# An encoder layer on one core: second chunk's squares first, third chunk's first weights on GpSimd's queue, late adaLN tiles beside the attention, last blocks' halves in turn

## The chip, the cores and the metric

The kernel runs on one core of a Trainium2 chip. A core has a matmul engine (TensorE, PE), VectorE (DVE), ScalarE (ACT), GpSimd (POOL) and SyncE (SP), which run side by side, each through its own program in order, and wait for each other by semaphores; DMA engines move data between the core's SBUF and memory. The metric is the time of one execution on the device in microseconds, lower is better. The kernel before was run three times, with 2073.9, 2080.23 and 2075.73 us (median 2075.73).

## The reference

One layer of an encoder on 2048 tokens of width 1024, all in fp32: modulated RMSNorm, windowed attention with 16 query heads, 4 key heads, a sink logit and a relative bias, then a SwiGLU feed-forward (FFN) of hidden width 2816. Shift, scale and gate of each half come from a vector `c` by one matrix (adaLN).

```python
mod = silu(c) @ ada_w + ada_b            # 6 x 1024: shift, scale, gate for two halves
h = rmsnorm(x) * (1 + scale1) + shift1
q, k, v = split(h @ w_qkv)
logits = q @ k_band.T / 8 + bias         # each block of 128 queries sees 3 blocks of keys
p = softmax(concat([masked(logits), sink]))[..., :-1]
x = x + gate1 * rmsnorm((p @ v_band) @ w_o)
h2 = rmsnorm(x) * (1 + scale2) + shift2
gate, up = split(h2 @ w_in)
x = x + gate2 * rmsnorm((silu(gate) * up) @ w_out)
```

## The kernel before

Every fp32 factor is split in a high and a low part (`split`, lines 149 to 151: ScalarE casts, another engine subtracts), and a product is three matmuls (`three`, L145 to L147). The tokens are worked on in four chunks of 512 with the features on the partitions.

By time: up to about 65 us the first chunk's norm, and its first seven QKV tiles (`NORD[:WAVE]`) one input tile k after the other, as the weights land. To 172.6 the rest of the first chunk and all of the second, with both sets of weights resident: `w1`-pool tiles hold the first seven tiles' columns (printed `w0_k`), `w2` the other five (printed `w1_k`). To about 783 the attention: 64 units (four chunks, four key heads, four blocks of 128 queries), each a score step (`scores`: matmuls L509, softmax L512 on VectorE, L514 on ScalarE, L518 on GpSimd) and, two units later, a value step (`values`: transposes L531, matmuls L536 and L537). Between units a generator gives 17.9 matmuls' worth of filling work (`Budget`): the QKV of the third and fourth chunk (`fill_qkv`, weights loaded again as `wsr`, split to `ws`), then the output projection of finished blocks (`TokenBlock`). To about 1640 the FFN's first matrix, by blocks of seven products of sums (`Hidden`, `Block.step`), in two halves of 1024 tokens; then the second matrix to the end.

A scheduler puts each engine's program in an order of its own, by a timeline that it keeps; `tc.issue_after(x)` holds an instruction back behind `x` in that order, and pools decide what memory a tile shares with earlier ones. SP issues nearly all loads and stores, and at most eight of its DMAs are under way, since eight semaphores go round: a DMA waits until the one eight before, SP's or ScalarE's, has landed.

What the change touches:

- `Chunk.squares` (L176): ScalarE squares eight tiles, two engines in turn add them up (L186). For the second chunk it is called behind the seven evacuations and behind the second set of weights (`w_piece(k, 1)`, splits on GpSimd, L151). `norm` sums over the features by matmuls with ones (`nsta`, L121), either on the fp32 sums (`direct`) or on a split of them.
- `late_ada` (L380): 24 adaLN tiles of 512 KB beyond the first 16 are loaded on GpSimd's queue beside the QKV of two chunks, and reduced on VectorE (L298).
- The pools of the attention (L428): the bias tables lie in memory opened first, the probability buffers `pr` after them. GpSimd clears `pr` (L456).
- `last_blocks` (L842): the last two token blocks of the output projection, two halves of 24 matmuls each, block after block, and behind each block its two RMSNorms and stores of `x1_d` and `n_d` (`ends`, on ScalarE's queue).
- `give_pair` (L911): from two hidden tiles by two halves it makes the operands of the second matrix; two of its subtractions (L934, L938) run on GpSimd.

Of the kernel before, what the change touches and what calls it, by code (L numbers as in the profile page):

```python
# [17 lines left out]
P = 128  # L18
# [49 lines left out]
def encoder_layer(ctx, tc, a):  # L68
# [190 lines left out]
    with ExitStack() as pa:  # L259
# [37 lines left out]
        def ada_reduce(t, w):  # L297
            dve.tensor_tensor_reduce(w, w, cb, 1.0, adab[:, t:t + 1], ALU.mult, ALU.add, mod[:, t:t + 1])  # L298
# [26 lines left out]
        for k in range(KT):  # L325
            with tc.issue_after(steps[max(k - 2, 0)][0]) if k >= 1 else ExitStack():
                ada_reduce(*ada_load(8 + k, raws))
                shift = ada_load(k, raws)
                w_piece(k, 0)
            with tc.issue_after(steps[k - 1][1]) if k >= 1 else ExitStack():  # L330
                ada_reduce(*shift)
            dve.scalar_tensor_tensor(coef[:, 0, k:k + 1], mod[:, 8 + k:9 + k], 1.0, gains[:, 0, k:k + 1],
                                     ALU.add, ALU.mult)
            with tc.issue_after(steps[k - 2][1]) if k >= 2 else ExitStack():
                steps.append(ch0.h(k))
            for n in NORD[:WAVE]:
                three(pss[n], wres[k, n], ch0.hh[k], k == 0, k == KT - 1)
        for n in NORD[:WAVE]:
            evac(0, n, pss[n], psA, "mm")
# [5 lines left out]
        ch1 = Chunk(1)  # L345
        ch1.squares()

# [31 lines left out]
        waiting, left = [], list(range(2 * KT, 5 * KT))  # L379

        def late_ada(n, keep):
            with tc.issue_after(newest["norm"]):
                while len(waiting) > keep:
                    ada_reduce(*waiting.pop(0))
            for _ in range(min(n, len(left))):
                waiting.append(ada_load(left.pop(0), raws, pool))

        for i, n in enumerate(NORD[WAVE:]):
            qkv_tile(ch0, n)
            if i == 0:  # L390
                ch1.norm(psA, "mm", True)
            if i >= 1:
                ch1.h(2 * i - 2)
                ch1.h(2 * i - 1)
            if i >= 2:
                late_ada(2 + (i == 4), 2)
        for i, n in enumerate(NORD):
# [5 lines left out]
            if i == 5:  # L403
                ch2.norm(psA, "mm")
# [24 lines left out]
    qkv = open_pool(att, "qkv", 2, side="right")  # L429
    bp = open_pool(att, "bp", side="right")  # L430
    sm = open_pool(att, "sm", 4, side="right")
    pp = open_pool(att, "pp", side="right")
# [113 lines left out]

    def fill_qkv(ch, nxt):

        for i, n in enumerate([8, 9, 10, 11] + list(range(8))):
            ni = NORD.index(n)  # L550
            raw = wsr.tile([P, KT, P], F32, tag="raw", name=f"wsr{ch.c}_{n}")
            newest["wsr"] = sp.dma_start(raw, a["w_qkv"][:, :, ni * P:(ni + 1) * P].rearrange("k p c -> p k c")).ins
# [9 lines left out]
            if nxt is not None:  # L562
                if i == 0:
                    with tc.issue_after(newest["wsr"]):
                        nxt = nxt()
# [206 lines left out]

    units = [Unit(c, g, jb) for c in range(NCH) for g in range(KVH) for jb in range(JB)]
# [27 lines left out]
    weights = output_weights()  # L801
    for i, un in enumerate(units):
# [3 lines left out]
        if un.jb == 0 and i + JB < len(units):  # L806
            nx = units[i + JB]
            load_qkv(nx.c, nx.g)
        if 22 <= i < half:
            next(weights, None)  # L810
# [31 lines left out]
    def last_blocks(bs):  # L842

        blocks = [TokenBlock(NCH - 1, b, late=True) for b in bs]
        for x in blocks:
            for i in range(2):
# [4 lines left out]
            x.ends()  # L851
# [60 lines left out]
    def give_pair(hf, j):  # L912
# [19 lines left out]
        b11, b12, b21, b22 = (b[n] for n in ("b11", "b12", "b21", "b22"))  # L932
        give("b11", b11, True)
        pool.tensor_tensor(b11, b12, b11, ALU.subtract)  # L934
# [3 lines left out]
        pool.tensor_tensor(b22, b22, b11, ALU.subtract)  # L938
# [424 lines left out]
```

## Time and profile before

| | |
|---|---|
| profiled execution | 2078.2 us, its span 2076.4 |
| mean granted TensorE clock | 0.989 of full speed |
| TensorE busy | 2017.2 us, 97% of the span, 9412 matmuls |
| VectorE, ScalarE, GpSimd busy | 1505.6, 992.5 and 921.8 us |
| DMA | 398.49 MB, 192 GB/s in the mean |
| chain that ended last | TensorE 72%, VectorE 9%, DMA 9%, ScalarE 4% |

A busy share of TensorE counts a matmul that waits in its pipe as busy, so TensorE does less work in a stretch than it could even where little idle time shows. The granted clock has two levels, 1.2 GHz (0.5) and 2.4 GHz (1.0). In a table of stages each engine has its busy time with the number of its instructions; in a group by shape the columns are line, engine, operation, output and inputs, shapes and count, then busy time and the mean of one in ns, then the idle time before them and what ended it. A chain of waits is followed back from the end of a stretch: each piece has its start and length.

### The profile page before, as it was taken

The page shows a single profiled execution, that of the slowest core. Times are in us where ns is not written, and L with a number is a line of the kernel's source. Part 1 is how long each engine was busy: PE and PEld are TensorE (multiplying, and loading weights), DVE is VectorE, ACT ScalarE, POOL GpSimd, SP SyncE. Part 2 cuts the span into 40 slices and gives each one's busy share as a digit, 9 for nine tenths or more (in the row PEclk, how much of TensorE's full clock was granted, in tenths as well). Part 3 has the DMA queues.
Part 4 walks back from the last instruction along what each step waited for, and adds up shares of the span by engine and source line. Part 5 has one row for each costly group of instructions (what it writes and reads, how often), then busy time and mean ns, then how long its engine had stood idle before and what let it go on. Part 6 is the DMA issues. An engine that isn't in the chain of part 4 may idle for free.

```text
span 2076.4 us, 28772 instructions
## 1 busy us (share of the span) xinstructions
PE 2017.2 (97%) x9412; PEld 1660.0 (80%) x9412; DVE 1505.6 (73%) x2632; ACT 992.5 (48%) x2105; POOL 921.8 (44%) x915
## 2 busy tenths in 40 slices
PE   8898999999999998999999999999999999999998
PEld 6786788878887786888888887888888788888886
DVE  8767566657777668566676698777776699987656
ACT  4426667667777656333233343434333554453222
POOL 0414556444445635555665456545553333344300
PEclk9999999999999999999999999999999999999999
DMA  7889678674647575433743454544534454488663
GB/s 299 261 259 270 177 195 252 154 194 138 200 141 229 183 246 193 145 130 108 245 161 121 159 173 149 203 146 158 187 137 149 155 179 147 152 310 343 254 253 122
DMA packets 256645, 398.49 MB, mean 192 GB/s; under 512 B 85045, under 2 KB 135781, under 8 KB 254448
## 3 DMA queue, kind: packets, MB, share of 16 engines
q1 hardware_dynamic: 245776, 363.03, 53.8%
q0 software_dynamic: 4928, 16.85, 2.3%
q10 hardware_dynamic: 5792, 16.79, 2.1%
q8 instruction: 74, 1.21, 0.2%
q14 instruction: 75, 0.61, 0.1%
HBM read 267.83 MB, written 128.76 MB: 191 GB/s over the span
## 4 chain that ended last, share of the span: by engine, by line
PE 72%; DVE 9%; DMA 9%; ACT 4%; issue 3%; POOL 2%; SPq 1%; DVEq 0%; ACTq 0%; POOLq 0%
PE pc_i L147 12%; PE pc_i L146 12%; PE pc_i L145 12%; PE po L1215 5%; PE po L1216 5%; PE po L1217 5%; PE psq L147 3%; PE psq L145 3%; PE psq L146 3%; PE t L531 2%; PE s L509 2%; PE py L624 1%; PE py L625 1%; PE py L626 1%; PE o L537 1%
## 5 line engine op out<-in xcount | busy, mean ns | idle before, releaser
L145 PE MATMUL pc_i<-ht,ws_i 128*128 128x512 f32 x528 | 206.7, 392 | 4.9 <-ACT ht L150 4.9
L146 PE MATMUL pc_i<-ht,ws_i 128*128 128x512 f32 x528 | 207.3, 393 | 1.6 <-DVE ht L151 1.6
L147 PE MATMUL pc_i<-ht,ws_i 128*128 128x512 f32 x528 | 207.2, 392 | 0.0
L150 ACT CAST wa_i<-wiri 128x512 fp32r<-128x512 f32 x132 | 81.6, 620 | 217.0 <-DMA wiri<-w_in 118.1
L512 DVE CUSTOM_DVE_ANT_0 pr<-s,bias,nsink 128x288 f32<-128x288 f32 (+3 forms) x256 | 125.0, 500 | 81.5 <-PE s L509 70.0
L518 POOL TENSOR_SCALAR pr<-pr,rs 128x288 f32<-128x288 f32 (+3 forms) x256 | 130.3, 528 | 113.3 <-DVE rs L516 107.8
L514 ACT ACTIVATE pr<-pr,nm 128x289 f32<-128x289 f32 (+3 forms) x256 | 135.4, 531 | 60.6 <-DVE nm L512 54.9
L890 POOL TENSOR_TENSOR s_i<-wiri 128x512 f32<-128x512 f32 x44 | 61.0, 1387 | 197.7 <-DMA wiri<-w_in 168.2
L151 DVE TENSOR_TENSOR wa_i<-wiri,wa_i 128x512 fp32r<-128x512 f32 x132 | 128.1, 970 | 24.3 <-ACT wa_i L150 24.1
L1220 DVE TENSOR_TENSOR z<-po,z 128x512 f32<-128x512 f32 x164 | 110.7, 684 | 44.4 <-PE po L1217 42.6
L151 DVE TENSOR_TENSOR ws_i<-s_i,ws_i 128x512 fp32r<-128x512 f32 x132 | 127.1, 963 | 21.1 <-ACT ws_i L150 20.9
L145 PE MATMUL pc_i<-hb,wa_i 128*128 128x512 f32 x352 | 138.1, 392 | 0.0
L147 PE MATMUL pc_i<-hb,wa_i 128*128 128x512 f32 x352 | 137.7, 391 | 0.0
L146 PE MATMUL pc_i<-hb,wa_i 128*128 128x512 f32 x352 | 137.5, 391 | 0.0
L151 DVE TENSOR_TENSOR plo<-t,phi 128x512 fp32r<-128x512 f32 x184 | 122.0, 680 | 20.1 <-ACT phi L150 19.6
L1215 PE MATMUL po<-wo_s,g 128*128 128x512 f32 x320 | 124.2, 391 | 2.4 <-DVE z L1220 1.7
L1216 PE MATMUL po<-wo_s,g 128*128 128x512 f32 x320 | 124.8, 390 | 0.1
L1217 PE MATMUL po<-wo_s,g 128*128 128x512 f32 x320 | 124.5, 389 | 0.0
L531 PE MATMUL t<-ident,pr 128*128 128x128 f32 x736 | 118.4, 276 | 5.9 <-POOL pr L518 3.4
L509 PE MATMUL s<-k,q 128*128 128x288 f32 (+4 forms) x512 | 114.3, 319 | 9.3 <-DVE nm L512 7.7
L145 PEld LDWEIGHTS pc_i<-ht,ws_i 128*128 128x128 f32 x528 | 99.7, 189 | 27.2 <-ACT ht L150 5.3
L146 PEld LDWEIGHTS pc_i<-ht,ws_i 128*128 128x128 f32 x528 | 99.7, 189 | 23.7 <-DVE ht L151 1.9
(255 smaller groups left out, 5913.3 us busy)
## 6 DMA issues: line engine op xcount, KB each, us to landing
wiri<-w_in SPq DMA_DIRECT2D x88, 512.0 KB, 4.7
wr<-w_out SPq DMA_DIRECT2D x20, 1024.0 KB, 9.0
g<-g_d_t SPq DMA_DIRECT2D x36, 512.0 KB, 5.2
g<-g_d_b SPq DMA_DIRECT2D x35, 512.0 KB, 5.7
q_d<-eq SPq DMA_DIRECT2D x64, 256.0 KB, 5.0
q<-q_d SPq DMA_DIRECT2D x16, 1024.0 KB, 9.0
ada<-ada_w POOLq DMA_DIRECT2D x24, 512.0 KB, 6.4
wsr<-w_qkv SPq DMA_DIRECT2D x24, 512.0 KB, 5.4
```

The source lines that it names most:

```text
L145: pe.matmul(ps, w[0], h[0], start=first, stop=False)
L146: pe.matmul(ps, w[0], h[1], start=False, stop=False)
L147: pe.matmul(ps, w[1], h[0], start=False, stop=last)
L151: return eng.tensor_tensor(lo, src, f(hi), ALU.subtract).ins
L509: m = pe.matmul(ps[:, :n], qs, kk[:, e, jb * P + lo:jb * P + hi], start=e == 0, stop=e == 1)
L512: dve.tensor_tensor_reduce(pr[:, i, lo:hi], ps[:, :n], bias[g][:, lo - starts[i]:hi - starts[i]], -1.0, nsink[:, g:g + 1], ALU.add, ALU.mi ...
L514: act.activation(pr[:, i, lo:hi + 1], pr[:, i, lo:hi + 1], AF.Exp, bias=nm[:, i:i + 1], scale=-1.0, accum_out=rs[:, i:i + 1])
L518: pool.tensor_scalar(pr[:, i, lo:hi], pr[:, i, lo:hi], rs[:, i:i + 1], 1.0, ALU.mult, ALU.mult)
L531: pe.transpose(pt[:, i * P:(i + 1) * P], pr[:, i, jj * P:(jj + 1) * P], ident)
L1215: pe.matmul(ps, g[:, 0], w[:, 0], start=i < FRESH and k == 0, stop=False, **on)
L1216: pe.matmul(ps, g[:, 0], w[:, 1], start=False, stop=False, **on)
L1217: pe.matmul(ps, g[:, 1], w[:, 0], start=False, stop=k == m - 1, **on)
```

## The change

1. The second chunk's squares are added before the evacuations of the first seven tiles and before the second weights, all on GpSimd.
2. Eight of the 24 late adaLN tiles are loaded on SP into two buffers and reduced by a generator that is stepped beside every second unit from the fourth on; the other 16 wait for an earlier norm.
3. The third chunk's norm sums the fp32 squares directly.
4. `pr` is opened before the bias tables, so `pr` now lies over the first weights and the bias over the second.
5. The weights of the third and fourth chunk come from a copy in memory of another layout (`w_qkv_t`, 4 KB in one piece for each partition); the first two tiles, 8 and 9, go on GpSimd's queue ahead of the units. The fourth chunk is no longer held behind the second weight tile.
6. The last two blocks' halves are made in turn.
7. Where an operand is given in two parts, which is in the second half of the tokens, both GpSimd subtractions go to VectorE.

```diff
+        ch1 = Chunk(1)
+        ch1.squares((pool, pool))
         for n in NORD[:WAVE]:
             evac(0, n, pss[n], psA, "mm")
...
         for k in range(KT):
             w_piece(k, 1)
-        ch1 = Chunk(1)
-        ch1.squares()
...
-        waiting, left = [], list(range(2 * KT, 5 * KT))
+        waiting, left = [], list(range(2 * KT, 4 * KT))
         def late_ada(n, keep):
-            with tc.issue_after(newest["norm"]):
+            with tc.issue_after(first_norm[0]):
...
-                ch2.norm(psA, "mm")
+                ch2.norm(psA, "mm", True)
...
+    pp = open_pool(att, "pp", side="right")
     bp = open_pool(att, "bp", side="right")
     sm = open_pool(att, "sm", 4, side="right")
-    pp = open_pool(att, "pp", side="right")
...
+    def raw_weights(c, n, q=sp):
+        ni = NORD.index(n)
+        raw = wsr.tile([P, KT, P], F32, tag="raw", name=f"wsr{c}_{n}")
+        ins = q.dma_start(raw, a["w_qkv_t"][ni]).ins
+        if q is sp:
+            newest["wsr"] = ins
+        return raw
+
+    ahead_of_units = {(2, n): raw_weights(2, n, pool) for n in (8, 9)}
...
                 if i == 0:
-                    with tc.issue_after(newest["wsr"]):
-                        nxt = nxt()
+                    nxt = nxt()
...
+    def ada_beside():
+        todo = list(range(4 * KT, 5 * KT))
+        pend = [ada_load(todo.pop(0), ada_late) for _ in range(2)]
+        yield
+        while pend:
+            ada_reduce(*pend.pop(0))
+            if todo:
+                pend.append(ada_load(todo.pop(0), ada_late))
+            yield
...
+        if i % 2 and i >= 3:
+            next(beside, None)
...
-        for x in blocks:
-            for i in range(2):
+        for i in range(2):
+            for x in blocks:
...
-            x.ends()
+                if i:
+                    x.ends()
...
+        eng = dve if parted else pool
         give("b11", b11, True)
-        pool.tensor_tensor(b11, b12, b11, ALU.subtract)
+        eng.tensor_tensor(b11, b12, b11, ALU.subtract)
         dve.tensor_tensor(b12, b22, b12, ALU.subtract)
         give("t3", b12, False)
         give("b22", b22, True)
-        pool.tensor_tensor(b22, b22, b11, ALU.subtract)
+        eng.tensor_tensor(b22, b22, b11, ALU.subtract)
```

GpSimd's program from the second chunk's squares to the last split of the second weights (`w1_k`, of which the seven tiles' rest is made), before:

```order
L186 TENSOR_TENSOR normed_385<-normed_385,squared_384 128x512 x3
L151 TENSOR_TENSOR w1_4_859<-wqkv4_1_857,w1_4_859 128x640
L151 TENSOR_TENSOR w1_0_842<-wqkv0_1_447,w1_0_842 128x640
L294 DMA ada16_1083<-ada_w 128x1024
L151 TENSOR_TENSOR w1_1_846<-wqkv1_1_448,w1_1_846 128x640
L151 TENSOR_TENSOR w1_2_850<-wqkv2_1_449,w1_2_850 128x640
L151 TENSOR_TENSOR w1_3_854<-wqkv3_1_450,w1_3_854 128x640
L151 TENSOR_TENSOR w1_5_864<-wqkv5_1_862,w1_5_864 128x640
L151 TENSOR_TENSOR w1_6_869<-wqkv6_1_867,w1_6_869 128x640
L151 TENSOR_TENSOR w1_7_874<-wqkv7_1_872,w1_7_874 128x640
```

and now:

```order
L186 TENSOR_TENSOR normed_385<-normed_385,squared_384 128x512 x6
L151 TENSOR_TENSOR w1_4_890<-wqkv4_1_888,w1_4_890 128x640
L151 TENSOR_TENSOR w1_0_873<-wqkv0_1_447,w1_0_873 128x640
L151 TENSOR_TENSOR w1_1_877<-wqkv1_1_448,w1_1_877 128x640
L151 TENSOR_TENSOR w1_2_881<-wqkv2_1_449,w1_2_881 128x640
L186 TENSOR_TENSOR normed_385<-normed_385,squared_384 128x512
L151 TENSOR_TENSOR w1_3_885<-wqkv3_1_450,w1_3_885 128x640
L151 TENSOR_TENSOR w1_5_895<-wqkv5_1_893,w1_5_895 128x640
L151 TENSOR_TENSOR w1_6_900<-wqkv6_1_898,w1_6_900 128x640
L151 TENSOR_TENSOR w1_7_905<-wqkv7_1_903,w1_7_905 128x640
```

Before, three additions stand there (the other four on VectorE); now six stand ahead of the first split and the seventh behind the fourth.

SP's program at the end of the second chunk's QKV (`q_d`, `v_d`: stores and loads of queries and values; `x3`: the fourth chunk; `wor`: output weights; `wsr`: weights of the third chunk), before:

```order
L450 DMA bias3_1975<-tab_d_357 32x288 x2
L237 DMA q_d1_2_66<-eq1_2_1486 1024x1x64 x4
L728 DMA wor0_0_3971<-w_o 128x2x512
L728 DMA wor0_1_3973<-w_o 128x2x512
L237 DMA q_d1_3_67<-eq1_3_1693 1024x1x64 x4
L480 DMA v0_0_1787<-v_d1_0_96 128x128
L480 DMA v0_1_1836<-v_d1_1_97 128x128
L552 DMA wsr2_8_1843<-w_qkv 128x8x128
L175 DMA x3_0_1912<-xT 128x512
L175 DMA x3_1_1913<-xT 128x512
```

and now, from the first table of the bias on:

```order
L450 DMA bias0_1770<-tab_d_357 32x288
L237 DMA q_d1_3_67<-eq1_3_1665 1024x1x64 x4
L450 DMA bias0_1770<-tab_d_357 32x288 x3
L450 DMA bias1_1804<-tab_d_357 32x288 x4
L450 DMA bias2_1870<-tab_d_357 32x288 x4
L175 DMA x3_7_1893<-xT 128x512
L450 DMA bias3_1947<-tab_d_357 32x288 x4
L244 DMA k_d2_0_84<-e2_8_1881 64x1024
L244 DMA k_d2_1_85<-e2_8_1881 64x1024
L550 DMA wsr2_10_2012<-w_qkv_t 128x1024
L294 DMA ada32_2053<-ada_w 128x1024
L294 DMA ada33_2055<-ada_w 128x1024
```

The first two weight tiles are gone from SP (they are the two DMAs on GpSimd's queue), the bias tables stand behind the last stores of queries instead of earlier, and the late adaLN tiles come between weight tiles.

VectorE's program from the last evacuations of the second chunk (`eq1_3`; now those of the third chunk's first two tiles, `e2_8` and `e2_9`) to the softmax of the first units (`nmB_G` is block B of key head G), before:

```order
L232 SCALAR_TENSOR_TENSOR eq1_3_1693<-psq1_7_1704,eq1_3_1693 128x16x32
L298 ISA ada37_1409,mod_358<-ada37_1409,normed_385,adab_359 128x1024
L298 ISA mod_358 128x1
L512 ISA pr_0_1778,nm0_0_1799<-s0_0_0_1802,bias0_1794,nsink_361 128x256
L512 ISA nm0_0_1799 128x1
L512 ISA pr_0_1778,nm0_0_1799<-s0_0_1_1807,bias0_1794,nsink_361 128x224
...
L151 TENSOR_TENSOR plo0_0_2_1998<-t0_0_2_1992,phi0_0_2_1997 128x512
L298 ISA ada38_1445,mod_358<-ada38_1445,normed_385,adab_359 128x1024
L298 ISA mod_358 128x1
L512 ISA pr_2_1780,nm2_0_1946<-s2_0_3_1964,bias0_1794,nsink_361 128x288
```

and now:

```order
L151 TENSOR_TENSOR e2_8_1881<-psq2_8_1822,e2_8_1881 128x512
L151 TENSOR_TENSOR e2_9_1992<-psq2_9_1905,e2_9_1992 128x512
L512 ISA pr_0_1750,nm0_0_1775<-s0_0_0_1778,bias0_1770,nsink_361 128x256
...
L298 ISA ada32_2053,mod_358<-ada32_2053,normed_385,adab_359 128x1024
L298 ISA mod_358 128x1
L512 ISA pr_2_1752,nm2_0_1918<-s2_0_2_1931,bias0_1770,nsink_361 128x288
L298 ISA ada33_2055,mod_358<-ada33_2055,normed_385,adab_359 128x1024
...
L298 ISA ada34_2260,mod_358<-ada34_2260,normed_385,adab_359 128x1024
L298 ISA ada35_2466,mod_358<-ada35_2466,normed_385,adab_359 128x1024
L541 TENSOR_TENSOR of0_0_1976<-o0_0_1952,low0_0_1975 64x4x128
...
L298 ISA ada36_2664,mod_358<-ada36_2664,normed_385,adab_359 128x1024
```

Before, two reductions stand between the softmax steps of the third unit; now the first softmax step stands behind two evacuations of filling work, and six reductions stand among the steps of the third and fourth unit (two more behind them, tiles 38 and 39).

## Rows read from the trace of the kernel before

**Rows 1.** Stages: us, busy time by engine, TensorE clock, DMA share, GB/s

```profile
60.00:80.00 20.00, 14.81 (x64) 11.81 (x63) 9.38 (x10) 10.96 (x19) 18.35 (x19) 0.74 0.77 241
172.00:224.00 52.00, 40.97 (x206) 32.33 (x205) 36.98 (x107) 36.52 (x97) 31.11 (x53) 0.93 0.89 250
780.00:800.00 20.00, 11.88 (x39) 8.58 (x38) 16.48 (x35) 16.92 (x34) 0.55 (x1) 0.83 0.81 296
800.00:1260.00 460.00, 459.11 (x2047) 378.66 (x2048) 321.84 (x401) 164.86 (x287) 270.04 (x179) 1.00 0.45 151
1280.00:1480.00 200.00, 200.00 (x879) 164.76 (x878) 158.01 (x212) 80.52 (x142) 104.19 (x74) 1.00 0.46 163
```

**Rows 2.** Chain of waits, 40 to 85 us: start, length, what

```profile
49.86 1.71 DVE x L209
...
53.44 0.67 DVE x L209
54.11 0.60 DVE normed L186
...
69.83 4.21 DVE normed L186
74.08 2.08 PE nsta L121 x2
```

**Rows 3.** GpSimd in order of time from 59 us: start, length, instruction

```profile
59.38 1.30 POOL L186 TENSOR_TENSOR normed<-normed,squared 128x512 f32<-128x512 f32 x1 [2.86 <-ACT squared L185]
60.64 3.11 POOL L151 TENSOR_TENSOR w<-wqkv,w 128x640 fp32r<-128x640 f32 x2
...
64.38 9.10 POOL L151 TENSOR_TENSOR w<-wqkv,w 128x640 fp32r<-128x640 f32 x6
```

**Rows 4.** Stages as in rows 1, the two halves of the first seam

```profile
68.00:74.00 6.00, 1.79 (x8) 1.34 (x6) 5.17 (x3) 1.73 (x4) 6.00 (x5) 0.59 0.89 249
74.00:80.00 6.00, 5.92 (x23) 4.84 (x24) 1.35 (x4) 2.44 (x4) 4.37 (x9) 0.56 0.37 82
```

**Rows 5.** Chain of waits, 165 to 225 us

```profile
172.86 4.03 POOL pr L456 x3
177.10 0.45 DVE pr L512
...
193.43 0.44 SPq L552
...
212.58 2.76 POOL ws L151
...
223.99 0.44 PE t L531 x4
```

**Rows 6.** Groups by shape, 172 to 224 us, four engines

```profile
L509 PE MATMUL s<-k,q 128*128 128x288 f32 x48 | 11.6, 351 | 1.9 <-DVE nm L512 1.8
L531 PE MATMUL t<-ident,pr 128*128 128x128 f32 x62 | 11.1, 288 | 2.2 <-DVE plo L151 1.0 <-POOL pr L521 1.0 <-POOL pr L518 0.2
L146 PE MATMUL psq<-h,ws 128*128 128x512 f32 x17 | 7.4, 437 | 0.0
...
L537 PE MATMUL o<-plo,v 128*128 128x512 f32 x13 | 5.6, 428 | 0.2 <-DVE plo L151 0.2
...
L298 DVE CUSTOM_DVE_ANT_0 ada<-ada,normed,adab 128x1024 f32<-128x1024 f32 x4 | 5.1, 1278 | 0.0
...
L150 ACT CAST ws<-wsr 128x1024 fp32r<-128x1024 f32 x4 | 4.2, 1044 | 3.1 <-DMA wsr<-w_qkv 3.1
...
L151 POOL TENSOR_TENSOR ws<-wsr,ws 128x1024 fp32r<-128x1024 f32 x4 | 10.0, 2490 | 4.3 <-ACT ws L150 4.3
```

**Rows 7.** DMA issues of the whole run: KB each, median us to landing

```profile
ada<-ada_w POOLq DMA_DIRECT2D x24, 512.0 KB, 6.4
```

**Rows 8.** Chain of waits, 765 to 800 us

```profile
782.16 4.01 DMA n_d<-xr
```

**Rows 9.** Groups by shape, VectorE, 1270 to 1640 us

```profile
L935 DVE TENSOR_TENSOR u_i<-u_i,u_i 128x512 f32<-128x512 f32 x8 | 5.5, 693 | 10.3 <-POOL u_i L983 10.3
```

More of the change, by code (lines that the diff above doesn't have):

```diff
@@ L391, in encoder_layer @@
                 ch1.norm(psA, "mm", True)
+                first_norm = [newest["norm"]]
             if i >= 1:
@@ L545, in values @@
                          of.rearrange("d (e i) t -> d e (i t)", e=2))
+    def raw_weights(c, n, q=sp):
[6 more added lines that the diff above has]
+    ahead_of_units = {(2, n): raw_weights(2, n, pool) for n in (8, 9)}
     def fill_qkv(ch, nxt):
         for i, n in enumerate([8, 9, 10, 11] + list(range(8))):
-            ni = NORD.index(n)
-            raw = wsr.tile([P, KT, P], F32, tag="raw", name=f"wsr{ch.c}_{n}")
-            newest["wsr"] = sp.dma_start(raw, a["w_qkv"][:, :, ni * P:(ni + 1) * P].rearrange("k p c -> p k c")).ins
+            raw = raw_weights(ch.c, n) if (ch.c, n) not in ahead_of_units else ahead_of_units[ch.c, n]
             w = ws.tile([P, 2, KT, P], F32R, tag="w", name=f"ws{ch.c}_{n}", bufs=2)
@@ L801, in encoder_layer @@
     weights = output_weights()
+    beside = ada_beside()
     for i, un in enumerate(units):
@@ L1345 @@
         "w_qkv": np.asarray(att_w_qkv)[0].reshape(KT, P, NQ, P)[:, :, NORD].reshape(KT, P, QKV_N),
+        "w_qkv_t": np.asarray(att_w_qkv)[0].reshape(KT, P, NQ, P)[:, :, NORD].transpose(2, 1, 0, 3),
         "x": np.asarray(x)[0].reshape(NCH, JB, P, D),
```

## The prediction

> **What bounds the kernel now.** I read the table of stages first [rows 1]. The reader is to see that TensorE has no idle time where weights stream through the FFN: 459.11 of 460 us from 800 to 1260 and 200 of 200 later, at a granted clock of 1.00. A change elsewhere that takes work from VectorE or GpSimd in those stretches is worth nothing, and so is one that adds some there as long as VectorE stays below its limit (158.01 of 200). Time can only be won at the seams. Three of them are touched: 60 to 80 us (TensorE 14.81 of 20, clock 0.74), 172 to 224 (40.97 of 52, clock 0.93) and 780 to 800 (11.88 of 20, clock 0.83). Then I read the chain of waits at each seam for what ends last, and the groups by shape there for the price of one instruction.
>
> In the first seam the chain runs through one addition of the second chunk's squares: it stands on VectorE from 69.83 for 4.21 us where another took 0.60, and `nsta`, the matmul that sums the squares, starts at 74.08 [rows 2]. It ended with GpSimd's six back-to-back weight splits (64.38, 9.10 us) [rows 3]. So TensorE did 1.79 us of work between 68 and 74, and the 6 us behind it ran at 0.56 [rows 4]. In the second seam the chain goes from the last QKV matmul through three memsets of the probability buffers (4.03 us), short softmax steps, a queue of SP stores that lets go the first of the third chunk's weights only at 193.43, and GpSimd's split of the second at 212.58 [rows 5]. In the third it goes through VectorE and ScalarE handing small pieces of RMSNorm to each other, then the store of `n_d` that SP's next operand load stands behind, 4.01 us [rows 8].
>
> **The change part by part.**
>
> *Squares first* (`ch1.squares((pool, pool))` ahead of the evacuations). All seven additions go to GpSimd, six ahead of its first weight split, the last behind the fourth. The loads set when the sixth can run, as now, so the first split still starts at 60.64. Two splits, one DMA issue (to 64.38), two splits of 1.56, one addition of 1.30: done at 68.8, and `nsta` may start there instead of at 74.08 [rows 2, 3]. Of 68 to 74 TensorE idled 4.2 us; the last split ends 1.3 later than now, which takes 1.2 of that back, as the matmuls behind follow GpSimd's splits. Of the 2.6 us that the half clock costs from 74 to 80 (6 x 0.44) I count 1.5 as won, since TensorE no longer stops first [rows 4]: 4.5 in all. Against it: VectorE's step L209 took 1.71 us while a GpSimd addition ran and 0.67 without [rows 2], and four more additions move there, while four of 0.60 leave VectorE: 4 x 1.04 - 2.4 = 1.8 later at worst, on VectorE's chain that leads to this point. I take 0.5 of it. **Gain 4**, between a loss of 1.8 and a gain of 6.8 (4.2 + 2.6). From 80 to 172 TensorE is full, so the gain is carried to the attention. There the third chunk's norm by the fp32 ones-matmul costs TensorE up to 2.08 us at half clock, so 1.04 at full [rows 2], less two matmuls of 0.22: **0.6 lost**.
>
> By the Trainium skill, page "SBUF — State Buffer", section "Who interferes with whom", a VectorE instruction with two SBUF inputs contends with a GpSimd instruction that reads SBUF, and the second to issue waits until the first is through. The 4.21 us addition agrees, so by that rule every moved addition is a lock of about 1.3 us; by it alone this part would come out at 1.8 lost, which is the second rival below.
>
> *The attention's start.* What TensorE does in 172 to 224, at its steady pace (459.11/2047 = 0.224 us for 512 columns [rows 1]; four transposes 0.44 [rows 5]): 64 score matmuls of 17,152 columns (48 of 288, 16 shorter of 208 in the mean), 54 of `psq` (17 of each form, one less of the third, and the second chunk's last four) and 26 of `o`, 25.4 us, and 62 transposes, 6.8 [rows 6]. 32.2 of 52: 19.8 are lost. After the change the memsets of `pr` go, since `pr` lies over the first weights, which are done long before. The two weight tiles come on GpSimd's queue ahead of the units, so 48 matmuls are there early. But their ScalarE cast stands behind the last evacuation: 172.6, then 0.7 for that (a like step [rows 9]), 1.05 for the cast and 2.49 for the split [rows 6] make 176.8; TensorE has 1.8 us of work until then and loses 2.4. The two tiles end at about 186.9. Only then does VectorE get to the first softmax step, behind both evacuations: 187.6 at the earliest, where it now starts at 177.10 [rows 5]. And the bias, now loaded over the second weights after the last QKV matmul, comes behind `q_d` stores; it stands two groups of stores ahead of that 193.43, I put it near 185, so this wait is just covered.
>
> From here VectorE's own order is the limit. All eight adaLN reductions stand in the first five units, in pairs, and the buffers hold two. The first load stands on SP behind the same stores and the biases; SP is now through the stores at 193.43 [rows 5], and with the biases in place of other loads I put the issue at 192, the landing 6.4 later [rows 7]: 198.4, reduced by 199.7. Tile 34 is only loaded then: 206. With 35 behind it (1.28 each [rows 6]) and eight steps of 0.5 to 0.7, unit 3's last score matmul is released at about 212. Between 186.9 and 212 TensorE's order holds 28 scores (3.5), 20 transposes (2.2), four `o` (0.9) and one tile of 24 (5.4): 12.0 of 25.1, so 13.1 lost. Two more such pairs (36 and 37, 38 and 39) follow, hidden in part by the next tile's 24 matmuls; I count 3. That makes 2.4 + 13.1 + 3 = 18.5 against 19.8: **gain 1.3**. Ends: if VectorE never waits for those loads, the 13.1 falls to about 6 and the gain is 8; if each pair costs a whole trip (6.4 + 1.3) with nothing beside it, three of them are 23, which is 13 lost.
>
> *Last blocks in turn.* The number of rounds between VectorE and ScalarE stays five; block 2's second half is done 5.4 us later and block 3's first half earlier, so one round of block 2 moves beside block 3's. What goes is one link: the tenth operand load no longer waits for the `n_d` store that landed 4.01 after 782.16, but for the `x1_d` store before it [rows 8]. **Gain 1.5**, between a loss of 3 and a gain of 4.
>
> *The subtractions.* Nine pairs give 18 to VectorE, 0.69 each like its own subtraction there [rows 9], 12.4 us. TensorE is full there and VectorE at 79% [rows 1], so this hides: **0**, and 12.4 lost only if VectorE became the bound; nothing gained.
>
> *The rest* (weights in 4 KB pieces, third norm's squares earlier, 4 MB of adaLN out of the stretch 80 to 172): hidden by a full TensorE; 0, with 2 either way for the later units.
>
> Sum: 4 - 0.6 + 1.3 + 1.5 = 6.2 less. From the profiled execution's 2078.2 that is 2072.0. It lies 2.5 above the median of the runs shown, 2075.73, so the forecast on their scale is 2069.5.
>
> **The rivals.**
>
> *The units start without a second wait.* The loads of the pairs come in time because SP has little else to do there; the attention's start gains 8, the squares 5: 13.9 with the rest (5 - 0.6 + 8 + 1.5), so 2061.8. For it: fill work is there early, and 19.8 us is much to take from. Against it: a pair's load is issued only when the pair before is reduced.
>
> *VectorE pays for the squares.* The wave ends later by as much as the addition saves: the squares lose 1.8, the rest stands: 0.5 less, 2075.2. For it: 1.71 against 0.67. Against it: the additions are spaced by the loads, and GpSimd is idle then.
>
> *Slower: the adaLN trips.* Place: VectorE between unit 0 and unit 5. With two buffers, tiles 34, 36 and 38 each wait a load that starts after a reduction, and on SP the load of 36 stands behind weights that wait for GpSimd's split; the softmax steps queue behind each. Price: 13 lost there, so 13 - 4 + 0.6 - 1.5 = 8.1 more: 2083.8. The whole turns slower once the time lost up to the fifth unit passes 24.7 us, the 19.8 of now and the 4.9 that the other parts win.
>
> **How the numbers follow.** About 0.3%, 6.2 us, can be told from no change here. Forecast 0.45, and it lies right at that bound: 0.22 faster, 0.23 same. First rival 0.21, all faster. Second 0.16, same but for 0.01. Third 0.18: 0.15 slower, 0.03 same. Faster 0.43, same 0.41, slower 0.16. The range goes from 2058, somewhat under the first rival, to 2083.
>
> **What would show it.** `nsta` of the second chunk near 69 instead of 74, the stretch 60 to 80 some 4 us shorter, all QKV work ending near 168.5. In the units: the first softmax step about 15 us after the last QKV matmul instead of 4.5, waits of VectorE at L298 for adaLN loads, and 18 us lost instead of 20 up to the fifth unit. At the FFN's start TensorE's wait for `ht` about 1.5 shorter. TensorE without waits in the second half of the FFN. I am wrong if the last QKV matmul has not moved, or if the units' start is shorter or longer by more than 7 us.

## The result and the profile after

The changed kernel took 2087.28 us (median of five, 2085.13 to 2090.19), the kernel before 2075.66 (five, 2073.9 to 2080.23): 1.0054 times as long, with a 95% interval of 1.0038 to 1.007, so 11.6 us slower where 6.2 less were forecast. Measured again beside other kernels it was 3.7 and 5.8 us slower. The sign is sure; the size differs between measurements, since single executions of it range from 2071.9 to 2090.2 us.

The table of stages of the changed kernel, columns as in [rows 1]; its QKV work ends at 175.31, 2.9 us later than before:

```profile
40.00:60.00 20.00, 15.21 (x57) 11.87 (x56) 19.87 (x24) 6.19 (x10) 8.36 (x5) 0.83 0.29 93
60.00:80.00 20.00, 20.00 (x107) 16.79 (x107) 9.52 (x15) 12.28 (x20) 17.63 (x16) 1.00 0.91 282
100.00:120.00 20.00, 17.22 (x57) 11.27 (x57) 15.74 (x30) 7.74 (x15) 3.56 (x7) 0.83 1.02 305
172.00:224.00 52.00, 40.24 (x180) 31.31 (x179) 31.16 (x66) 28.06 (x66) 24.72 (x25) 0.87 0.79 238
224.00:335.00 111.00, 100.58 (x511) 82.69 (x510) 86.10 (x187) 70.94 (x168) 58.32 (x83) 0.97 0.68 189
780.00:800.00 20.00, 16.00 (x63) 12.56 (x62) 13.71 (x31) 13.47 (x33) 5.12 (x4) 0.91 0.82 292
```

The same view of the kernel before, for three stretches that the prediction didn't look at:

```profile
40.00:60.00 20.00, 18.17 (x77) 14.06 (x76) 18.97 (x29) 7.91 (x13) 4.37 (x3) 1.00 0.40 132
100.00:120.00 20.00, 20.00 (x84) 15.19 (x83) 12.99 (x22) 6.59 (x12) 2.13 (x4) 1.00 1.05 330
224.00:335.00 111.00, 109.80 (x566) 91.32 (x565) 71.82 (x160) 72.11 (x162) 66.19 (x78) 1.00 0.72 195
```

The first seam itself is mended: from 60 to 80 TensorE works 20.00 of 20 at full clock, where it did 14.81 at 0.74 [rows 1, 4]. The last row stands 11 us earlier in the program than its counterpart, so it is not compared. But the 20 us ahead of it are worse (57 matmuls instead of 77, VectorE busy 19.87 of 20), 100 to 120 is newly broken, and from 172 to 335 TensorE gets through 691 matmuls instead of 772. Its granted clock is lower there too: 0.87 from 172 to 224 (before 0.93 [rows 1]) and 0.97 from 224 to 335 (before 1.00), which comes to about 20 us at the half level where it was 7.

What VectorE does in the worse 20 us, in the changed kernel's chain of waits, columns as in [rows 2]:

```profile
42.77 1.28 DVE ada L298
...
44.72 2.11 DVE w L151
46.83 2.20 DVE ada L298
...
52.05 1.00 DVE w L151
...
54.38 2.25 DVE ada L298
```

Equal steps stand there at 1.28 and 2.20, and at 1.00 and 2.11: the long ones are those beside GpSimd's additions (three from 44.22 to 50.16, one from 54.26). TensorE waits for the step behind them (its waits from 40 to 120 us: us in total, times, longest):

```profile
PE psq L146 <- DVE h L217: 7.5, 2, 4.8
```

At the attention's start, SP's program in order of time in the changed kernel:

```profile
181.00 0.37 SPq L450 DMA_DIRECT2D bias<-tab_d  x1
181.47 4.46 SPq L237 DMA_DIRECT2D q_d<-eq  x4
185.97 6.95 SPq L450 DMA_DIRECT2D bias<-tab_d  x11
...
196.58 0.55 SPq L550 DMA_DIRECT2D wsr<-w_qkv_t  x1
197.17 1.47 SPq L294 DMA_DIRECT2D ada<-ada_w  x2
```

The bias lies over memory that the QKV work holds to its end, so its first row is issued at 181.00 (before: 149.0), the first softmax step follows at 191.9, 16.6 us behind the last QKV matmul (before: 3.2), and the first late adaLN tile is issued only behind all that. VectorE in order of time (in brackets the idle time before and what ended it), and what its eight adaLN reductions waited for in all (us, times):

```profile
200.06 0.08 DVE L512 DVE_READ_ACCUMULATOR2_ANT nm<- 128x1 f32 x1
203.64 3.09 DVE L298 CUSTOM_DVE_ANT_0 ada<-ada,normed,adab 128x1024 f32<-128x1024 f32 x1 [3.50 <-DMA ada<-ada_w]
...
206.66 0.51 DVE L512 CUSTOM_DVE_ANT_0 pr<-s,bias,nsink 128x288 f32<-128x288 f32 x1
```

```profile
  DMA ada<-ada_w: 8.2, 3
```

VectorE is done with a softmax step at 200.1, and the matmuls of the next are through at about 200.3; it runs at 206.66. The loads themselves are no slower than [rows 7] (KB each, median us to landing, 185 to 330 us):

```profile
ada<-ada_w SPq DMA_DIRECT2D x8, 512.0 KB, 6.4
```
TensorE's first wait from 168 to 335 us, first in the changed kernel, then before:

```profile
PE s L509 <- DVE nm L512: 15.5, 11, 2.3
```

```profile
PE s L509 <- DVE nm L512: 5.1, 5, 1.5
```

### The profile page after: what moved, and what is told of

Read it like the earlier page. It is cut to its first block, busy times and chain, and to the rows that moved or that the text cites. A ratio compares the mean times of both kernels' runs of the same rounds, so it can differ in the third digit from the quotient of the medians.

```text
span 2088.4 us, 28761 instructions
## 1 busy us (share of the span) xinstructions
PE 2020.0 (97%) x9412; PEld 1663.2 (80%) x9412; DVE 1516.7 (73%) x2644; ACT 995.7 (48%) x2105; POOL 903.9 (43%) x895
## 4 chain that ended last, share of the span: by engine, by line
PE 75%; DVE 9%; DMA 7%; issue 3%; ACT 3%; SPq 2%; POOL 1%; DVEq 0%; ACTq 0%; POOLq 0%
PE pc_i L147 12%; PE pc_i L146 12%; PE pc_i L145 12%; PE po L1238 5%; PE po L1237 5%; PE po L1239 5%; PE t L531 3%; PE s L509 2%; PE psq L147 2%; PE psq L146 2%; PE psq L145 2%; PE o L536 1%; PE o L537 1%; PE py L631 1%; PE py L632 1%
## 5 line engine op out<-in xcount | busy, mean ns | idle before, releaser
L151 DVE TENSOR_TENSOR wa_i<-wiri,wa_i 128x512 fp32r<-128x512 f32 x132 | 139.4, 1056 | 14.2 <-ACT wa_i L150 13.8
L151 DVE TENSOR_TENSOR ws_i<-s_i,ws_i 128x512 fp32r<-128x512 f32 x132 | 117.9, 893 | 30.8 <-ACT ws_i L150 30.5
L150 ACT CAST ws_i<-s_i 128x512 fp32r<-128x512 f32 x132 | 81.8, 620 | 84.5 <-PE pc_i L147 80.7
L145 PEld LDWEIGHTS pc_i<-ht,ws_i 128*128 128x128 f32 x528 | 99.4, 188 | 25.4 <-ACT ht L150 4.0
```

The source lines that it names most:

```text
L145: pe.matmul(ps, w[0], h[0], start=first, stop=False)
L150: act.copy(hi, src)
L151: return eng.tensor_tensor(lo, src, f(hi), ALU.subtract).ins
```

## The experiments

"Lost" is the length of a stretch less what its matmuls take at the steady pace (0.227 us for 512 columns, 0.109 for a transpose), worked out from each trace; "start" is the 160 us behind the last QKV matmul, "attention" the start and the rest up to the last projection matmul. A matmul at the half clock counts as time lost as well. Each trace is one execution: the three of the changed kernel (changed, c2, c4) differ by 2.9 us at the start and by about 5 in the two columns beside it. The execution traced lies 5.5 us under its kernel's median in a3 and 10.5 above it in b2. Runs between two lines were made together, on one chip.

| kernel | median us (n) | before beside it | ratio [95%] | QKV ends | lost 40–80 | 80–QKV end | start | attention |
|---|---|---|---|---|---|---|---|---|
| before | 2075.7 (5) | | | 172.4 | 12.6 | 2.9 | 25.2 | 58.9 |
| changed | 2087.28 (5) | 2075.66 | 1.0054 [1.0038, 1.007] | 175.3 | 8.0 | 9.2 | 38.6 | 67.0 |
| --- | | | | | | | | |
| a1_squares_back | 2075.15 (12) | 2076.42 | 0.9995 [0.9984, 1.0005] | 173.4 | 12.5 | 3.0 | 31.9 | 58.1 |
| a2_ada_back | 2082.39 (12) | 2076.42 | 1.0029 [1.0013, 1.0045] | 170.9 | 8.7 | 4.5 | 36.8 | 64.9 |
| a5_units_as_before | 2076.95 (12) | 2076.42 | 1.0006 [0.9993, 1.0018] | 170.7 | 7.8 | 4.8 | 32.8 | 64.3 |
| b4_squares_pool | 2072.59 (12) | 2076.42 | 0.9978 [0.9966, 0.9989] | 170.1 | 8.6 | 3.8 | 30.7 | 55.1 |
| --- | | | | | | | | |
| c1_hold_x2 | 2079.85 (12) | 2075.99 | 1.0014 [0.9999, 1.003] | 169.6 | 8.7 | 2.8 | 36.6 | 63.3 |
| c2_after_again | 2079.74 (12) | 2075.99 | 1.0026 [1.0007, 1.0044] | 170.7 | 8.0 | 5.3 | 35.7 | 61.8 |
| b1_blocks_only | 2079.65 (12) | 2075.99 | 1.0013 [0.9999, 1.0027] | 172.5 | 12.2 | 2.8 | 22.3 | 59.2 |
| b2_subs_only | 2074.76 (12) | 2075.99 | 0.9992 [0.9974, 1.001] | 171.8 | 11.7 | 2.9 | 28.0 | 64.0 |
| --- | | | | | | | | |
| a3_pools_back | 2070.62 (12) | 2074.42 | 0.9975 [0.9959, 0.9991] | 168.9 | 8.2 | 3.8 | 25.1 | 54.0 |
| a8_ada_later | 2074.49 (12) | 2074.42 | 0.9998 [0.9984, 1.0011] | 171.1 | 8.3 | 5.0 | 25.4 | 60.0 |
| c4_after_third | 2080.2 (12) | 2074.42 | 1.002 [1.0003, 1.0036] | 170.4 | 8.7 | 4.3 | 37.7 | 64.6 |
| b5_squares_subs | 2068.84 (8) | 2074.42 | 0.9967 [0.995, 0.9984] | 167.2 | 7.7 | 2.7 | 30.6 | 57.5 |
| --- | | | | | | | | |
| a9_both | 2058.81 (5) | 2076.99 | 0.9912 [0.9897, 0.9927] | 171.0 | 8.3 | 5.1 | 19.0 | 47.3 |
| a10_both_hold | 2056.47 (5) | 2076.99 | 0.9906 [0.9891, 0.9922] | 168.5 | 8.0 | 2.8 | 17.7 | 44.8 |
| a11_both_hold_no_blocks | 2053.93 (4) | 2076.99 | 0.989 [0.9872, 0.9908] | 169.1 | 8.0 | 3.0 | 17.5 | 39.3 |

**a1_squares_back.** The changed kernel with the squares as before.

```diff
-        ch1 = Chunk(1)
-        ch1.squares((pool, pool))
         for n in NORD[:WAVE]:
...
             w_piece(k, 1)
+        ch1 = Chunk(1)
+        ch1.squares()
```

> The changed kernel with the second chunk's squares put back behind the evacuations and the second weights, GpSimd and VectorE in turn. Theory 1 (the squares on GpSimd lengthen VectorE's steps before 60 us and so cost more than they win): the wait of psq for VectorE's h (4.8 us at 40 to 62) goes, nsta is back at 74, and the QKV ends about 3 us earlier than in the changed kernel (172.4 instead of 175.3); time about 2084. Rival (the QKV's loss comes from the stall near 97 us alone, which the squares do not make): nsta at 74, the stall near 97 stays, the QKV ends at 177 or later, time 2087 to 2090.

Both missed the time: without the early squares the change costs nothing, and the start loses 31.9 instead of 36 to 39, though the long wait for `h` is gone and `nsta` is back at 74.7, as theory 1 had it. Yet the squares alone (b4) win. So the loss is not the early squares' by themselves.

**a2_ada_back.** All 24 adaLN tiles beside the QKV again.

```diff
-        waiting, left = [], list(range(2 * KT, 4 * KT))
+        waiting, left = [], list(range(2 * KT, 5 * KT))
-            with tc.issue_after(first_norm[0]):
+            with tc.issue_after(newest["norm"]):
...
-        if i % 2 and i >= 3:
-            next(beside, None)
```

> The changed kernel with all 24 late adaLN tiles loaded and reduced beside the QKV, as before, none beside the units. Theory 1 (VectorE's waits for adaLN loads between units 0 and 5 are what the units lose): the waits of VectorE at L298 after 188 us go, and time falls by 5 to 8 us, to about 2080 to 2082. Rival (the units lose because softmax stands behind filling work and the bias comes late): time falls by at most 2 us, 2085 to 2088, TensorE still waits for VectorE's nm between 188 and 212.

The median met the first theory's number, but the changed kernel had no run beside it: measured later it lay 3.7 and 5.8 us above the kernel before, and this one lies 6.0 above, so nothing that can be told was won. The waits for adaLN loads are gone and another has come. In GpSimd's program the third chunk's weights now stand behind the adaLN loads and additions of squares and are issued at 184.91, so nothing covers the late bias. TensorE's waits, 165 to 200 us:

```profile
PE s L509 <- DVE nm L512: 23.3, 2, 20.3
```

**a5_units_as_before.** As a2, and the pools and the weights ahead as before too; squares, blocks and subtractions stay.

```diff
-    ahead_of_units = {(2, n): raw_weights(2, n, pool) for n in (8, 9)}
+    ahead_of_units = {(2, n): raw_weights(2, n, pool) for n in ()}
```

> The changed kernel with three of its edits taken back: the adaLN tiles beside the QKV, the bias pool ahead of pr, and no weights ahead of the units. Squares, direct norm, layout of the weights, last blocks and subtractions stay changed. Theory 1 (squares +3, units +8, last blocks +1.5): time about 2079, 8 us below the changed kernel. Rival (the squares and what follows them in the QKV cost nearly everything, the units only shift): time stays above 2084.

Equal to the kernel before: the first theory's side. The units' part is needed for the loss. The third norm, the weights' layout and the fourth chunk's earlier loads stay in it; no run takes one of them back alone.

**b4_squares_pool.** The kernel before with only the early squares (the hunk of a1, the other way).

> The kernel before with the second chunk's squares early and all on GpSimd, nothing else. Theory 1: TensorE waits near 50 us for VectorE's h as in the changed kernel, nsta near 72, and the time is 1 to 4 us above before (2077 to 2080). Rival (squares alone win, the stall near 97 us comes from the moved adaLN loads): QKV ends 2 us or more earlier than before, time 2071 to 2074.

The rival is right: 3.8 us won, which the forecast had put at 4. The wait that theory 1 named is there as well (4.8 us for `h`), and the part wins in spite of it.

**c1_hold_x2 and c2_after_again.** In the changed kernel ScalarE's first square of the third chunk stands ahead of evacuations that TensorE needs, and waits for its load. From 80 to 100 us, ScalarE's groups by shape (idle time last):

```profile
L182 ACT ACTIVATE normed<-x 128x512 f32<-128x512 f32 x1 | 0.6, 633 | 9.2 <-DMA x<-xT 9.2
```

The experiment queues these squares behind the first chunk's last evacuation; the other run is the changed kernel as it is.

```diff
-                ch2.squares((dve, dve))
+                with tc.issue_after(newest["aevac"]):
+                    ch2.squares((dve, dve))
```

> The changed kernel, with one edit more: ScalarE's squares of the third chunk are queued behind the first chunk's last evacuation, so that they cannot stand ahead of the evacuations of v. Theory 2 (with the squares early, ScalarE's order puts the first square of the third chunk, which waits 9 us for its load, ahead of evacuations, and the changed kernel crosses the slack there): TensorE's wait of 2.7 us near 104 and the half clock from 106 go, the QKV ends near 169 to 170 instead of 175.3, time 5 us or more below the changed kernel, 2082. Rival (that stall is one execution's chance, the units lose the rest): QKV ends between 170 and 171 in both, time within 2 us of the changed kernel run again.

> The changed kernel once more, unchanged, beside the others on the same chip. Theory 2: the QKV ends near 175 again, with TensorE's wait near 104, and time is 10 to 13 us above before. Rival (chance of one execution): the QKV ends near 171, and the profile's loss sits in the units.

The stall goes (idle time at L182: 9.2, in c2 8.1; with the hold 0 in a10), the loss from 80 us to the end of the QKV falls from 5.3 to 2.8, and the time doesn't move: the rival. The changed kernel itself came out 7.5 us faster than at first, with the QKV ending at 170.7, so the 175.3 of the first trace is not the rule.

**b1_blocks_only and b2_subs_only.** One part alone in the kernel before.

```diff
-        for x in blocks:
-            for i in range(2):
+        for i in range(2):
+            for x in blocks:
```

> The kernel before with the last two blocks' halves in turn, nothing else. As predicted: TensorE's waits at 780 to 800 shrink, 1 to 2 us faster (2074). Rival (the rounds between VectorE and ScalarE only move; what the second operand's loads win is lost by a second stall behind it): within 1 us of before, a second half-clock stretch after 800.

```diff
+        eng = dve if parted else pool
-        pool.tensor_tensor(b11, b12, b11, ALU.subtract)
+        eng.tensor_tensor(b11, b12, b11, ALU.subtract)
```

> The kernel before with the 18 subtractions on VectorE, nothing else. As predicted: no change within 1 us. Rival (at the change between the two halves of the FFN, near 1265, TensorE waits for what GpSimd's subtractions hold up): the 4.35 us lost from 1260 to 1280 shrink to under 1, and the time falls by 3 to 4 us.

The blocks in turn don't win. TensorE's waits from 725 to 825 us with them:

```profile
PE pc_i L145 <- ACT p_i L955: 3.5, 1, 3.5
PE py L624 <- ACT ol L150: 2.7, 1, 2.7
PE pc_i L145 <- ACT ht L150: 2.2, 1, 2.2
PE pc_i L146 <- DVE ht L151: 0.6, 2, 0.4
```

and before, from 730 to 830:

```profile
PE pc_i L145 <- ACT ht L150: 4.9, 1, 4.9
PE pc_i L145 <- ACT p_i L954: 2.5, 1, 2.5
PE pc_i L146 <- DVE ht L151: 1.6, 1, 1.6
```

9.0 us on both sides: the last block's first half now comes 24 matmuls earlier and waits for the attention output that it needs (`ol`). With the clock counted it is worse: over the 60 us from the first matmul of these four halves, the time lost as in the table is about 12 in the kernel before and 14 here; it is 14 to 17 in all traces with the halves in turn and 11 to 13 in those with the old order, but for 17 in b2's. The subtractions alone are no change that can be told.

**a3_pools_back, a8_ada_later, c4_after_third.** The two suspects at the start, undone one at a time, beside the changed kernel: the late bias, and the adaLN trips, which are the loads and reductions of the eight late tiles among the first units. First:

```diff
-    pp = open_pool(att, "pp", side="right")
     bp = open_pool(att, "bp", side="right")
     sm = open_pool(att, "sm", 4, side="right")
+    pp = open_pool(att, "pp", side="right")
```

> The changed kernel with the bias tables and the probability buffers in their old places (bias over the first weights, loaded beside the QKV; pr over the second, cleared by GpSimd), all else as changed. In the traces so far the first softmax step stands 16 us after the last QKV matmul with the new places and 3 us with the old; TensorE's time lost from that matmul to 160 us later is 38.6 and 35.7 us in two traces of the changed kernel, 25.2 before. Theory 1 (late bias): the first softmax step 3 to 5 us after the last QKV matmul, 26 to 30 us lost, and the median 5 to 8 us under the changed kernel run beside it. Rival (adaLN trips): the loads of the eight tiles set the pace whenever the softmax starts; 33 to 38 lost, the median within 3 us of the changed kernel's.

Second:

```diff
-            dve.reciprocal(rs, rs)
+            self.soft = dve.reciprocal(rs, rs).ins
...
-        if i % 2 and i >= 3:
-            next(beside, None)
+        if i % 2 and i >= 11:
+            with tc.issue_after(units[i - 1].soft):
+                next(beside, None)
```

> The changed kernel with the eight late adaLN tiles stepped beside the 12th to the 28th unit, each reduction held behind a softmax there, instead of beside the first five units. Theory 1 (late bias): the units' start still loses 33 us or more in 160, median within 3 us of the changed kernel run beside it. Rival (adaLN trips, the third rival of the prediction): the start loses 25 to 29 us, the median 5 to 8 us under the changed kernel's.

> The changed kernel unchanged, a third time, beside the two above. Its two medians so far lay 11.6 and 3.7 us above the kernel before, its executions from 2073.9 to 2090.2 us. Theory 1 (one kernel with a wide spread): again 3 to 8 us above the kernel before, and a spread of 10 us or more. Rival (the first measurement was another condition of the chip): within 3 us of the kernel before.

Each takes the loss away: 9.6 and 5.7 us under the changed kernel, which was slower a third time, with a spread of 15 us. The waits for `nm` from 168 to 335 us, for a3, then a8:

```profile
PE s L509 <- DVE nm L512: 2.5, 3, 1.5
```

```profile
PE s L509 <- DVE nm L512: 2.2, 3, 1.8
```

Neither theory alone holds; both causes are there. In a3 the first softmax step stands 1.9 us behind the last QKV matmul, in a8 still 19.2, and the start loses 25 in both. The two are linked by SP's program. In a3, which still reduces the eight tiles beside the first units, the first two loads go out 9 us behind the last QKV matmul, and 22 behind it in the changed kernel:

```profile
178.28 1.12 SPq L294 DMA_DIRECT2D ada<-ada_w  x2
```

and none of the eight reductions waits for its load. So the waits for the loads came with the late bias; what the reductions cost without them is VectorE's time among the softmax steps.

**b5_squares_subs.** The kernel before with early squares, the hold and the subtractions.

> The kernel before with the squares first on GpSimd, the third chunk's ScalarE squares queued behind the last evacuation of the first chunk, and the subtractions on VectorE; units, pools, weights and last blocks as before. Alone the squares gave 2072.59 (3.8 us less), the subtractions 2074.76 (1.2 less, within the spread). Theory 1: they add up, 2070 to 2072. Rival (the chance of the executions decides): 2074 to 2076.

2068.84, 5.6 us less: theory 1, the parts add up.

**a9_both, a10_both_hold, a11_both_hold_no_blocks.** Both causes undone in the changed kernel (the edits of a3 and a8), then the hold of c1 with it, then the blocks as before (the edit of b1, the other way).

> The changed kernel with the pools in their old places and the eight adaLN tiles beside the 12th to the 28th unit. Against the kernel before beside it, the pools back alone measured 3.8 us less, the later tiles alone the same, the changed kernel 5.8 more. Theory A (two causes that add up): another 4 to 6 us under the pools back alone, 8 to 10 us under the kernel before, the start losing 19 to 22 us in the 160 behind the last QKV matmul (25.1 with the pools back alone). Theory B (one loss, that the late bias and the adaLN trips make only together): within 2 us of the pools back alone, 2 to 6 under the kernel before, the start losing 24 to 27.

> As the one before, and ScalarE's squares of the third chunk queued behind the last evacuation of the first chunk. Theory A: the stall of 1 to 2 us between 100 and 120 us goes, and the median is 1 to 2 us lower than without. Theory B: TensorE's loss from 80 us to the last QKV matmul falls to 2.8 as it did before, but the end stays within 1 us.

> As the one before, with the last two blocks one after the other as in the kernel before. Theory A (the halves in turn cost something, as their run alone with 3.7 us more says): 2 to 4 us lower than the run before this. Theory B (that was the chance of the executions; the stages around 780 us show at most 1.4 us of difference, in favour of the halves in turn): within 1.5 us, or up to 1.5 slower.

All three medians lie on theory A's side, and the first goes far beyond its 8 to 10 us: without the late bias and the trips the rest of the change is worth 18.2 us, where the two single steps lead one to expect 9.5. In its trace 1.4 us of that lie up to the last QKV matmul, 6.2 at the start, 5.4 in the rest of the attention and about 6 behind it. The hold gives 2.3 and the old blocks 2.5 more, each within the spread of so few executions, so neither step is shown by the times. The last, 2053.93, is the fastest, 23 us under the kernel before. The sums of busy times over 172 to 224 and 224 to 335 us show the start; c4, a3, a8, a9 in this order:

```profile
sum 163.00, PE 145.86 PEld 118.16 DVE 116.37 ACT 99.25 POOL 85.49; mean PE 72.93 PEld 59.08 DVE 58.19 ACT 49.63 POOL 42.74
```

```profile
sum 163.00, PE 153.02 PEld 126.90 DVE 122.54 ACT 111.27 POOL 102.74; mean PE 76.51 PEld 63.45 DVE 61.27 ACT 55.63 POOL 51.37
```

```profile
sum 163.00, PE 152.83 PEld 126.37 DVE 107.25 ACT 104.85 POOL 89.21; mean PE 76.42 PEld 63.19 DVE 53.63 ACT 52.43 POOL 44.60
```

```profile
sum 163.00, PE 156.13 PEld 129.44 DVE 115.12 ACT 110.06 POOL 95.80; mean PE 78.07 PEld 64.72 DVE 57.56 ACT 55.03 POOL 47.90
```

And SP in a9, in order of time: eight bias rows go out while the QKV still runs:

```profile
147.36 8.13 SPq L450 DMA_DIRECT2D bias<-tab_d  x8
```

## Why the prediction was wrong

*The step that failed* is the attention's start: "That makes 2.4 + 13.1 + 3 = 18.5 against 19.8: gain 1.3". Its events were right: the first softmax step about 15 us after the last QKV matmul (measured 16.3 to 17.8 in three traces), the first adaLN load issued at 192 (192.0 in c4, 197.2 in the first trace), waits of VectorE for these loads, the first weights covering the wait for the bias. Its terms were too small. The first 60 us lose 22.3 to 23.9 (before: 20.3) where 2.4 + 13.1 was put; the 100 behind them lose 13.4 to 14.7, and 4.9 before, so "I count 3" for the two later pairs should have been about 9. I took the later pairs' waits as hidden for the most part by the next tile's 24 matmuls; the trace shows TensorE standing 11 times for `nm` (15.5 us) where it stood five times (5.1).

The third rival named the mechanism, with 13 lost and 2083.8; it had a chance of 0.18. Measured against the kernel before, the start is 10.5 to 13.4 longer in three traces, but only 2.0 to 3.6 of that lie in the first 60 us, which reach past the fifth unit, the last that this rival and the forecast looked at. The rest lies behind them, where the last of the eight reductions has started (226 to 234 us) and `nm` is still late. a8, which moves the reductions away, loses only about 6 there, and a3, without the late bias, about 9, so both are in it; how the delay is handed on from unit to unit no run shows. What the rival left out is that it takes the late bias as well: a3 keeps the reductions, and the start loses no more than before.

A second thing was put at nothing without a reason: the clock. The sum for the start takes every matmul at the steady pace. In the 160 us of the start TensorE stood at the half level for 7 us before and for 17 to 27 in the three traces; at half the pace that costs at most 5 to 10 us more. No run separates it from the waits, but a sum of waits alone leaves it out.

*The bias.* "This wait is just covered" was true for TensorE's first idle time and false for what follows: for 16 us VectorE does no softmax, and SP issues the adaLN loads only behind the bias rows, so the units start with nothing in hand when the trips come. At the start the two losses help each other: against c4's 37.7, undoing either takes away more than 12 us and undoing both 18.7. The times say the opposite: undoing one is worth 9.6 or 5.7, and both 24.0 (from 5.8 above the kernel before to 18.2 under it), 9 more than the sum. The start doesn't account for that, and it stays open how much of it is the chance of the executions or the chips.

*Squares first.* "I take 0.5 of it" (of VectorE's 1.8 us) failed: TensorE waits 4.8 us at once for VectorE, the additions lengthen adaLN reductions and weight splits too, not only L209, and the clock falls to its half level there for 3.4 to 6.8 us. The other half, the seam itself, gave more than forecast (20.00 of 20). `nsta` came at 71.98, not near 69. From 40 to 80 us the two errors nearly cancel, which is luck: the traces with the early squares lose 3.9 to 4.9 less there than the kernel before, where the terms gave 4. Some of it is lost again by 172: the last QKV matmul came 1.3 to 3.5 us earlier in eight of nine traces with the early squares and without the hold. The part alone measured 3.8 less in time. The Trainium skill's rule that I set beside the row (page "SBUF — State Buffer", section "Who interferes with whom") is the better guide for the length of VectorE's steps: the trace agrees, 2.11 beside 1.00 for a split. For the part's worth it was not: by it alone I had 1.8 lost. And the addition of 4.21 us agrees with it less well than I wrote, since it waited for more than one instruction: it ended 0.6 us behind the last of three of GpSimd's splits of 1.5 us.

*The rest, 0.* "Hidden by a full TensorE" failed in one place: the third chunk's earlier squares made ScalarE stand 9.2 us ahead of evacuations. It cost up to 6 us to the QKV's end in the first trace, 1 to 2.5 in the others (c1 against c2, a10 against a9).

*Last blocks, gain 1.5*: the link that I named did go (the wait for `ht` fell from 4.9 to 2.2), but 2.7 of waiting for `ol` and one more for `p_i` took its place; the step didn't ask when the last block's input is ready. By the traces the halves in turn lose some 2 to 5 us there (b1 against the kernel before, a10 against a11); the times of these runs don't show it clear of their spread.

*Subtractions, 0*: right by the time alone. At the changeover of the FFN's halves TensorE's wait was 2.6 us before, 2.0 with the subtractions alone and 2.7 in the changed kernel's first trace, but 0.3 to 1.1 in the twelve other traces with them. There the half-clock stretch behind the wait goes too (1230 to 1330 us: clock 0.98 and 421 matmuls before, 1.00 and 438 in c2), so in those traces "nothing gained" missed about 3 us.

*Not forecast:* behind the start the attention loses less in nearly all traces with the squares or the units' part (22 to 32 us; before 33.7, b1 and b2 36.9 and 36.0, but a8 34.6). No run says why. Why a1, with the late bias and the trips, loses only 31.9 at the start is not settled either.

## What to carry to other kernels

Count a moved buffer by when its new place comes free: swapping two pools delayed one small table by 32 us and was worth 9.6. Loads through two buffers, each issued after the reduction before, belong where the consumer has work in hand, not at a seam. And where several parts are changed at once, measure them apart: as a whole they were 4 to 12 us slower, while without the two bad placements and the blocks in turn, and with ScalarE's squares held back, they were 23 us faster than before.

## What the runs showed of the hardware

- An adaLN reduction on VectorE (accumulating, 128x1024) took 1.28 us, 2.20 and 2.25 beside GpSimd's additions, and 3.09 at 203.64, where a GpSimd split of 2.37 us ran from 203.27.
- One kernel's executions on one chip spread over 16 us (c2: 2073.9 to 2090.1) with equal instructions. The first two traces of the changed kernel, 15.5 us apart, differ by 1 us in ScalarE's wait for the third chunk's first tile, and show 69 us in all at the half clock against 45.
